# A three-block transformer kernel on one core: VectorE keeps the running sums of its depthwise convolution in PSUM

## The chip, the cores and the metric

The kernel runs on one core of a Trainium2 chip. The metric is the device time of one execution in microseconds (us), median of several runs. PE is the matrix engine (TensorE), DVE is VectorE, ACT is ScalarE, POOL is GpSimd, SP issues most DMAs. SBUF is the large on-chip memory, PSUM the eight banks of 128 partitions x 2 KB into which PE writes its sums.

## The reference

A sequence of 512 tokens of width 1024 goes through three layers, all in float32: one with a short convolution and latent attention, one with a conformer convolution (each of these two followed by a squared-ReLU MLP), and one with forgetting attention, pooling and a gated MLP. The change lies in the second:

```
def conformer_conv(h, w_pw1, b_pw1, w_dw, b_dw, ln_g, ln_b, w_pw2, b_pw2):
    u = h @ w_pw1 + b_pw1
    a, g = jnp.split(u, 2, axis=-1)
    u = a * jax.nn.sigmoid(g)
    u = depthwise_conv(u, w_dw) + b_dw      # 31 taps along the tokens, per channel
    u = jax.nn.silu(layer_norm(u, ln_g, ln_b))
    return u @ w_pw2 + b_pw2
```

## The kernel before, in words

Activations lie with 128 channels on the partitions and the 512 tokens along a partition, so the width of 1024 is eight channel tiles, c = 0 to 7. Every product is made of three fp32r matmuls of a head and a rest (`mm3`, L336 to L338). Weights are streamed: SP loads raw blocks, ACT makes the head (L264), DVE the rest (L265, which reads the raw block and the head, both in SBUF). Three raw buffers hold two blocks each; splitting is at most a few blocks ahead of PE.

In `conformer`, PE computes for each channel tile the two halves `za` and `zg` of `pw1` (two PSUM banks). `glu` then multiplies both by the norm's factor (DVE L1136, L1137: PSUM and SBUF in, SBUF out), ACT takes the sigmoid, and DVE L1139 makes the padded tile `up` of 542 tokens in SBUF from two SBUF tiles. The convolution of the tile is shared out by the string `CONV = "VPVVPMEE"`:

- V (c = 0, 2, 3): DVE does all 31 taps. The first is a multiplication (L1087), each later one `dst = u * w + dst` (L1091, called a tap below), where `u` is a shifted view of `up`, `w` one weight per partition, and `dst` the output tile `vv[c]` in SBUF.
- P (c = 1, 4): ACT multiplies (L1099 the first, L1102 the others, into a small buffer of a pool of nine), POOL adds the product to `vv[c]` (L1103).
- M (c = 5): ten taps as P, the other 21 on DVE into a tile `part` in SBUF (L1089, then L1091), and DVE adds the two (L1171, the merge).
- E (c = 6, 7): PE, as matmuls with diagonal matrices. `up` is split into head and rest (ACT L1109, DVE L1110). The diagonals of c = 6 are made earlier, those of c = 7 by ACT (L1060) during this stage. ACT L1129 takes the sum out of PSUM.

The taps are background work. DVE's are in the list `bg`, those of ACT and POOL in `bg2`; `tick(n, n2)` takes n and n2 operations, in turn from the first two tiles of a list, after each half of a `pw1` tile and each group of diagonals, and `drain` takes the rest. When all eight tiles `vv` are there, the layer norm begins: PE sums them over the channels (L1179, in the order 0, 2, 6, 1, 7, 4, 3, 5), DVE subtracts the mean, ACT squares (L1194), PE sums the squares (L1195), for the two halves of the tokens one after the other. The PSUM pool has eight banks.

The taps on DVE before:

```
else:
    V.scalar_tensor_tensor(out=dst, in0=u, scalar=w, in1=dst, op0=OP.mult, op1=OP.add)
```

Of the kernel before, what the change touches and what calls it, by code (L numbers as in the profile page):

```python
# [21 lines left out]
T = 512  # L22
# [41 lines left out]
# ---------------------------------------------------------------- host layout  # L64
# [12 lines left out]
def make_plan():  # L77
    """Weight pieces in the order in which they are used: (matrix, k, column tile, width)."""
# [64 lines left out]
def steps(order):  # L143
    """The steps of an order as it is written: name or name*times."""
    for s in order.split():
        name, _, n = s.partition("*")
        for _ in range(int(n or 1)):
            yield name


def pieces(order, use):
    """Weight pieces in the order of the steps that use them first."""
    use = {name: list(u) for name, u in use.items()}
    return sum([use[name].pop(0) for name in steps(order) if use.get(name)], [])


def pack(plan):
    """Cuts the plan into blocks of up to 512 columns, and those into loads of two blocks, but for the first two."""
    blocks, cols = [[]], 0
    for piece in plan:  # L160
        if cols + piece[3] > 512:
            blocks.append([])
            cols = 0
        blocks[-1].append(piece)
        cols += piece[3]
    return [blocks[:1], blocks[1:2]] + [blocks[i:i + 2] for i in range(2, len(blocks), 2)]
# [57 lines left out]
# ---------------------------------------------------------------- chip  # L224


class Weights:
    """Streams the weight blocks in and splits each into a 12 bit head and the exact rest."""
# [40 lines left out]
    def more(self, limit):  # L269
        """Splits one block beyond what is due, up to a number of blocks ahead."""  # L270
        if self.nsplit < min(self.cur + 1 + limit, len(self.blocks)):
            self.advance(self.nsplit - self.AHEAD)
# [10 lines left out]
class Program:  # L283
# [10 lines left out]
    # -- storage  # L294
# [23 lines left out]
    def tick(self, n, n2):  # L318
        """Background work: n and n2 operations of the two lists of queues, from a list's first two in turn."""
        for qs, num in ((self.bg, n), (self.bg2, n2)):  # L320
            for i in range(num):
                while qs and not qs[0]:
                    qs.pop(0)
                if not qs:
                    break
                q = qs[1] if i % 2 and len(qs) > 1 and qs[1] else qs[0]
                q.pop(0)()
# [5 lines left out]
    # -- arithmetic  # L333
# [6 lines left out]
    def units(self, name, t, xs, ks=None):  # L340
        """One closure (ps, columns) per product of a weight piece."""
# [13 lines left out]
    def kouter(self, names, h, ps=None, cols=slice(0, T), hooks=None, extra=None, ks=None):  # L355
        """Several output tiles at once, an input tile after the other."""
# [13 lines left out]
    def split(self, p, src, scale=None, cols=T, rows=slice(0, 128)):  # L370
        """p = (head, rest) of src [* scale per partition]."""
# [12 lines left out]
    def rsqrts(self, jobs):  # L384
        """out = (s / n + eps) ** -0.5, with one Newton step, for each (s, n, out)."""
# [23 lines left out]
    # -- tables of the scalar engine  # L409
# [4 lines left out]
    def tables(self, name):  # L414
        """Has the scalar engine load a set of tables, behind the functions that need the one before."""
# [10 lines left out]
    def fn(self, name, **args):  # L426
        """An activation whose function needs a set of tables."""
        self.tables(name)
        ins = self.nc.scalar.activation(**args).ins  # L429
        if self.table_load is not None:  # L430
            self.after(ins, self.table_load)
        self.table_fns.append(ins)

    def colsum(self, acc, cols=T):
        """Sums of acc over the partitions, on every partition."""
# [19 lines left out]
    # -- constants  # L455
# [13 lines left out]
    def late_consts(self):  # L469
# [14 lines left out]
        # a query on the partitions, a key on the columns: later keys are out  # L484
# [4 lines left out]
        # a key on the partitions, a query on the columns: 32 queries before the first 96 keys,  # L489
        # which stand above the 32 keys before them  # L490
# [6 lines left out]
        # a key of the last 32 on the first partitions, a query on the columns  # L497
# [4 lines left out]
        # adds the second 32 partitions to the first  # L502
# [11 lines left out]
    def angles(self):  # L514
        """cos and sin of the rope angles, row p for frequency p % 16."""
# [23 lines left out]
    # -- attention parts that both blocks use  # L539
# [7 lines left out]
    def v_tile(self, ps, rows, scales=None):  # L547
        """Values of four (block, head) groups as [v | ones | v | ones ...], head and rest."""
# [19 lines left out]
    def max_rows(self, mx, q, rows):  # L568
        """Puts the negative of the row maxima (mx[:, 4 * head + block]) into a row of each q."""
# [13 lines left out]
    def head_jobs(self, q, slots, scale, engines):  # L583
        """Closures of one head: scores and exponentials per slot of keys, then values.
        A slot is a list of (keys, first query, mask or None, values' function), where keys are the products
        (stationary, plane of q) that make the scores."""
# [5 lines left out]
        def score(j):  # L592
            ps = self.PS()
            off = 0
            for keys, c0, mask, _ in slots[j]:
                o = ps[:, off:off + T - c0]
                m = keys[0][0].shape[-1]
                # few keys: a first mask opens all the rows
# [32 lines left out]
    def normalise(self, e, o):  # L631
        """Values of a pair of heads over their sums: the even head is on top of its sums, the odd below."""
# [5 lines left out]
        # the negative of 1 / s, with one Newton step  # L638
# [8 lines left out]
    def head_ops(self, job, ys, nslots):  # L647
        """Closures for the scores and for the values of the slots of all heads; job(n) gives head n."""
# [20 lines left out]
    def parts(self, name, t, xs, done, ks=None, step=2):  # L669
        """A product in closures of a few input tiles each; done(sums) runs after the last."""  # L670
# [15 lines left out]
    # -- block 1, layer 0, mixer  # L686
    def mla(self, first):
# [10 lines left out]
        # products of constants until the first data is there: they raise the array's clock  # L698
# [68 lines left out]
        # shared key rope on partitions 64..95  # L767
# [6 lines left out]
        # query rope, (head, frequency) on the partitions  # L774
# [15 lines left out]
        # rows of a head: (64 | rope 32 | -max or 1 | zeros) or (-max or 1 | zeros | rope 32 | 64)  # L790
# [114 lines left out]
    # -- residual and norms between the parts  # L905
    def boundary(self, x, m, acc, last, gi, nxt, first, extra=None):
        """The last three tiles of m, x += rms_norm(m, g[gi]) and the first tiles of the next part, in halves
        of the tokens: the norms of one half run next to the products of the other.
        first: names of the next part's first tiles.  Returns x, h (without its rstd), the first tiles' sums
        and a function that gives the rstd."""  # L910
# [83 lines left out]
    # -- squared relu mlp  # L994
# [45 lines left out]
    # -- conformer convolution  # L1040
    def diagonals(self, c, early):
        """The taps of a channel tile as diagonal matrices, head and rest: at once, or eight as they are used."""
# [33 lines left out]
    def conformer(self, x, h, ps4, rs, first):  # L1076
# [5 lines left out]
        def conv_dve(c, up, dst, taps, bias):  # L1082
            def tap(t):
                w, u = self.v("dw", 31 * c + t), up[:, t:t + T]
                if t == taps[0]:
                    if bias:
                        V.tensor_scalar(out=dst, in0=u, scalar1=w, scalar2=self.v("bdw", c), op0=OP.mult, op1=OP.add)  # L1087
                    else:
                        V.tensor_scalar(out=dst, in0=u, scalar1=w, scalar2=None, op0=OP.mult)  # L1089
                else:  # L1090
                    V.scalar_tensor_tensor(out=dst, in0=u, scalar=w, in1=dst, op0=OP.mult, op1=OP.add)  # L1091

            return [lambda t=t: tap(t) for t in taps]
# [37 lines left out]
        def glu(c, za, zg):  # L1131
# [11 lines left out]
            elif CONV[c] == "V":  # L1143
                self.bg.append(conv_dve(c, up, vv[c], range(31), True))
            elif CONV[c] == "M":
                part = self.S()[:, :T]
                self.bg2.append(conv_pool(c, up, vv[c], range(MIX)))
                self.bg.append(conv_dve(c, up, part, range(MIX, 31), False))
# [21 lines left out]
        for c, part in mixed:  # L1170
            V.tensor_add(out=vv[c], in0=vv[c], in1=part)  # L1171
        self.tables(RSQRT)
        # layer norm in halves of the tokens; the tensor engine has little else to do and adds float32 as it is
# [60 lines left out]
    # -- block 2  # L1234
    def meta_norm(self):
        """The meta tokens' first norm, complete: head and rest, channels on the partitions."""
# [11 lines left out]
        # the heads and 16 columns of zeros, the rests and as many  # L1248
# [7 lines left out]
        # tokens on the partitions, the rest zero: keys of two pairs and one tile of the pooled part  # L1256
# [4 lines left out]
    def meta_unit(self, ps, w, k):  # L1261
        """Tokens on the partitions; the second 32 partitions take the tokens' rests."""
# [7 lines left out]
    def forget_first(self):  # L1270
        """The keys of the meta tokens next to the first tiles' second half."""
# [10 lines left out]
    def forget(self, x, h, ps4, rs, pm2):  # L1282
        """Keys stand in tiles of 128: 96 in their order and the 32 before them; the first tile has the meta
        tokens and 16 empty keys there, and the last 32 keys are in a tile of their own, below 96 empty ones."""
# [14 lines left out]
        # the first plane has the head of a head's 64 and rows (-max | 1), twice (-1 | 8 cum), twice (8 cum | 1),  # L1299
        # a head and a rest each; the second plane has (rest | head) and (head | rest)  # L1300
# [81 lines left out]
        # z * rstd and its squares, split  # L1382
# [13 lines left out]
        # the meta tokens' keys, tokens on the partitions  # L1396
# [91 lines left out]
        # values of four heads  # L1488
# [165 lines left out]
    # -- gated mlp of block 2  # L1654
# [88 lines left out]
```

## Time and profile before

| | before |
|---|---|
| median of 3 runs (lowest to highest) | 1869.91 us (1869.52 to 1872.47) |
| span of the profiled execution, first to last instruction | 1867.9 us |
| the profiled execution's own time | not recorded apart from its span |
| PE busy | 1773.1 us (95%) |
| DVE busy | 1176.0 us (63%) |
| ACT busy | 828.6 us (44%) |
| POOL busy | 330.1 us (18%) |
| mean granted clock of PE | 0.973 |

The profile is of one execution, taken by the hardware profiler. A busy share is an average over the whole span; the slices and windows tell where an engine is busy. Times of instructions are durations; since an instruction may start before the one ahead of it has ended, the distance between two starts can be shorter. [...]

### The profile page before, as it was taken

Reading aid. Unit: us, or ns where it says so; the run is one execution under the profiler, and the core shown is the slowest. Engines: PE = TensorE matmul, PEld = TensorE weight load, DVE = VectorE, ACT = ScalarE, POOL = GpSimd, SP = SyncE. Lnnn points to the kernel's source line nnn. Section 1 sums busy time; section 2 is a strip of 40 time slices with the busy share of each in tenths; the row PEclk is TensorE's granted clock in tenths of the full one; section 3 lists DMA queues with packets and bytes.
Section 4 is the critical chain, followed back from the end, with each engine's and each line's share of the span. In section 5 each row is a group of like instructions: output and inputs, shape, how many; then the busy total and the mean of one; then the engine's idle time right before and its main releaser. Section 6 shows DMA issues by size and latency. Waiting matters only on the chain.

```text
span 1867.9 us, 22812 instructions
## 1 busy us (share of the span) xinstructions
PE 1773.1 (95%) x8630; PEld 1459.5 (78%) x8630; DVE 1176.0 (63%) x1786; ACT 828.6 (44%) x1531; POOL 330.1 (18%) x353
## 2 busy tenths in 40 slices
PE   9999979999999986839999999999999999999999
PEld 7778877888888865729888888887777888888887
DVE  7978695344444899985934443458988654344442
ACT  6546645333333544817644242436666433232231
POOL 3413270000000357820300000015122200000000
PEclk9999999999999998969999999999999999999999
DMA  5231313322222211002232232223221332332231
GB/s 200 70 96 50 102 46 113 99 93 90 101 92 79 86 39 55 14 22 69 91 100 94 90 102 90 93 87 104 59 81 53 117 102 90 94 98 91 93 99 57
DMA packets 47581, 158.83 MB, mean 85 GB/s; under 512 B 6592, under 2 KB 7040, under 8 KB 47472
## 3 DMA queue, kind: packets, MB, share of 16 engines
q1 hardware_dynamic: 45472, 152.31, 24.9%
q0 software_dynamic: 1936, 5.07, 0.9%
q8 instruction: 67, 1.10, 0.2%
q14 instruction: 42, 0.34, 0.1%
q10 hardware_dynamic: 64, 0.02, 0.0%
HBM read 149.86 MB, written 4.19 MB: 82 GB/s over the span
## 4 chain that ended last, share of the span: by engine, by line
PE 72%; DVE 20%; issue 3%; ACT 2%; POOL 1%; DMA 1%; SPq 0%; POOLq 0%; DVEq 0%; ACTq 0%
PE ps L337 23%; PE ps L336 23%; PE ps L338 23%; DVE P L1091 5%; DVE W L265 2%; DVE P L947 1%; DVE P L380 1%; DVE S L1091 1%; PE ps L602 1%; POOL P L950 1%; DVE S L1479 1%; ACT S L429 1%; DVE P L377 1%; DVE S L403 1%; PE ps L1195 1%
## 5 line engine op out<-in xcount | busy, mean ns | idle before, releaser
L338 PE MATMUL ps<-P,W 128*128 128x512 f32 (+1 forms) x2413 | 900.0, 373 | 16.6 <-DVE W L265 16.6
L337 PE MATMUL ps<-P,W 128*128 128x512 f32 (+1 forms) x2413 | 900.6, 373 | 8.5 <-DVE P L380 8.5
L336 PE MATMUL ps<-P,W 128*128 128x512 f32 (+1 forms) x2413 | 904.7, 375 | 2.2 <-ACT P L379 1.0
L265 DVE TENSOR_TENSOR W<-raw,W 128x512 fp32r<-128x512 f32 x546 | 399.0, 739 | 396.1 <-ACT W L264 391.9
L264 ACT ACTIVATE W<-raw 128x512 fp32r<-128x512 f32 x546 | 338.6, 629 | 681.0 <-PE ps L338 583.8
L338 PEld LDWEIGHTS ps<-P,W 128*128 128x128 f32 x2413 | 458.2, 190 | 105.4 <-DVE W L265 19.4
L337 PEld LDWEIGHTS ps<-P,W 128*128 128x128 f32 x2413 | 458.7, 190 | 95.1 <-DVE P L380 10.0
L336 PEld LDWEIGHTS ps<-P,W 128*128 128x128 f32 x2413 | 458.6, 190 | 90.2 <-ACT P L379 1.6
L950 POOL TENSOR_TENSOR P<-P 128x256 f32<-128x256 f32 x48 | 46.6, 979 | 798.7 <-DVE P L947 797.6
L377 DVE TENSOR_TENSOR P<-S,P 128x512 fp32r<-128x512 f32 (+1 forms) x130 | 91.0, 706 | 50.1 <-ACT P L376 49.3
L1103 POOL TENSOR_TENSOR P<-P,S 128x512 f32<-128x512 f32 x69 | 113.8, 1670 | 49.0 <-ACT S L1102 47.6
L1091 DVE SCALAR_TENSOR_TENSOR P<-P,vec 128x512 f32<-128x512 f32 x90 | 112.3, 1288 | 0.0
L376 ACT ACTIVATE P<-S 128x512 fp32r<-128x512 f32 (+1 forms) x130 | 78.9, 613 | 70.2 <-DVE S L1666 25.8
L1008 DVE SCALAR_TENSOR_TENSOR S<-ps,S 128x512 f32<-128x512 f32 x64 | 43.7, 690 | 37.3 <-PE ps L338 37.1
L379 ACT ACTIVATE P<-P,vec 128x256 fp32r<-128x256 f32 (+1 forms) x80 | 43.7, 550 | 50.3 <-POOL P L950 30.4
L449 POOL TENSOR_TENSOR S<-S 128x256 f32<-128x256 f32 (+1 forms) x45 | 48.1, 1070 | 76.3 <-ACT S L448 73.9
L380 DVE SCALAR_TENSOR_TENSOR P<-P,vec 128x256 fp32r<-128x256 f32 (+1 forms) x80 | 55.9, 712 | 8.3 <-ACT P L379 8.2
L336 PE MATMUL ps<-P 128*128 128x512 f32 (+4 forms) x134 | 53.0, 395 | 7.3 <-ACT P L1060 3.3
L337 PE MATMUL ps<-P 128*128 128x512 f32 (+4 forms) x134 | 53.3, 398 | 4.2 <-DVE P L1110 3.8
L338 PE MATMUL ps<-P 128*128 128x512 f32 (+4 forms) x134 | 52.9, 395 | 1.6 <-ACT P L1060 1.6
L615 POOL TENSOR_TENSOR P<-S,P 128x512 fp32r<-128x512 f32 (+1 forms) x24 | 34.3, 1428 | 112.5 <-DVE P L614 95.6
L448 ACT ACTIVATE S<-P 128x256 f32<-128x256 f32 (+1 forms) x105 | 46.4, 472 | 17.4 <-DVE P L1035 11.4
(270 smaller groups left out, 1464.2 us busy)
## 6 DMA issues: line engine op xcount, KB each, us to landing
raw<-in_w SPq DMA_DIRECT2D x270, 512.0 KB
P<-in_xT SPq DMA_DIRECT2D x8, 256.0 KB
P<-in_xT POOLq DMA_DIRECT2D x8, 256.0 KB, 5.7
keep<-P SPq DMA_DIRECT2D x8, 256.0 KB
P<-P SPq DMA_DIRECT2D x16, 128.0 KB
P<-keep POOLq DMA_DIRECT2D x8, 256.0 KB, 4.9
out<-P SPq DMA_DIRECT2D x7, 256.0 KB
raw<-in_w SPq DMA_DIRECT2D x2, 256.0 KB
```

What stands on the lines that cost most here:

```text
L264: nc.scalar.activation(out=w[:, 0, :cols], in_=r, func=AF.Copy)
L265: nc.vector.tensor_sub(out=w[:, 1, :cols], in0=r, in1=w[:, 0, :cols].bitcast(F32))
L336: mm(ps, w[0], x[0], start=first, stop=False)
L337: mm(ps, w[0], x[1], start=False, stop=False)
L338: mm(ps, w[1], x[0], start=False, stop=last)
L376: nc.scalar.activation(out=hi, in_=src, func=AF.Copy)
L377: nc.vector.tensor_sub(out=lo, in0=src, in1=hi.bitcast(F32))
L380: nc.vector.scalar_tensor_tensor(out=lo, in0=src, scalar=scale, in1=hi.bitcast(F32), op0=OP.mult, op1=OP.subtract)
L449: (eng or nc.vector).tensor_add(out=acc, in0=acc, in1=t)
L950: ins = eng.tensor_add(out=x[k][:, cols], in0=x[k][:, cols], in1=m[k][:, cols]).ins
L1091: V.scalar_tensor_tensor(out=dst, in0=u, scalar=w, in1=dst, op0=OP.mult, op1=OP.add)
L1103: G.tensor_add(out=dst, in0=dst, in1=p)
```

## The change

`conv_dve` takes a bank of the PSUM pool when a tile's first tap is issued and keeps the running sum there. The first tap writes the bank, every further tap reads and writes it, and only the last tap of a V tile writes `vv[c]` in SBUF. The M tile has no buffer `part` any more: its sum stays in PSUM, and the merge reads it there. The rest of the diff strips comments, and every line behind `conv_dve` is numbered higher by 6 (L1091 becomes L1096, L1087 and L1089 become L1091 and L1093; L1102, L1103 become L1108, L1109; L1110 L1116; L1136 L1142; L1171 L1177; L1179 L1185).

```diff
         def conv_dve(c, up, dst, taps, bias):
+
+            box = {}
+
             def tap(t):
                 w, u = self.v("dw", 31 * c + t), up[:, t:t + T]
                 if t == taps[0]:
+                    acc = box["acc"] = self.PS()
                     if bias:
-                        V.tensor_scalar(out=dst, in0=u, scalar1=w, scalar2=self.v("bdw", c), op0=OP.mult, op1=OP.add)
+                        V.tensor_scalar(out=acc, in0=u, scalar1=w, scalar2=self.v("bdw", c), op0=OP.mult, op1=OP.add)
                     else:
-                        V.tensor_scalar(out=dst, in0=u, scalar1=w, scalar2=None, op0=OP.mult)
+                        V.tensor_scalar(out=acc, in0=u, scalar1=w, scalar2=None, op0=OP.mult)
                 else:
-                    V.scalar_tensor_tensor(out=dst, in0=u, scalar=w, in1=dst, op0=OP.mult, op1=OP.add)
-
-            return [lambda t=t: tap(t) for t in taps]
+                    acc = box["acc"]
+                    V.scalar_tensor_tensor(out=dst if dst is not None and t == taps[-1] else acc, in0=u, scalar=w,
+                                           in1=acc, op0=OP.mult, op1=OP.add)
+
+            return [lambda t=t: tap(t) for t in taps], box
...
             elif CONV[c] == "V":
-                self.bg.append(conv_dve(c, up, vv[c], range(31), True))
+                self.bg.append(conv_dve(c, up, vv[c], range(31), True)[0])
             elif CONV[c] == "M":
-                part = self.S()[:, :T]
                 self.bg2.append(conv_pool(c, up, vv[c], range(MIX)))
-                self.bg.append(conv_dve(c, up, part, range(MIX, 31), False))
+                taps, part = conv_dve(c, up, None, range(MIX, 31), False)
+                self.bg.append(taps)
                 mixed.append((c, part))
...
         for c, part in mixed:
-            V.tensor_add(out=vv[c], in0=vv[c], in1=part)
+            V.tensor_add(out=vv[c], in0=part["acc"], in1=vv[c])
```

The order on DVE at the end of the convolution, from the second L1110 (after: L1116) on, before the change (P and S are tiles in SBUF, ps is a PSUM bank, vec the weights per partition; the last two rows shown then go on in turn up to the merge):

```order
L1110 TENSOR_TENSOR P<-P 128x542
L1091 SCALAR_TENSOR_TENSOR P<-P,vec 128x512 x15
L1089 TENSOR_SCALAR S<-P,vec 128x512
L1091 SCALAR_TENSOR_TENSOR P<-P,vec 128x512 x4
L1091 SCALAR_TENSOR_TENSOR S<-P,vec,S 128x512
L1091 SCALAR_TENSOR_TENSOR P<-P,vec 128x512
```

and of the change:

```order
L1116 TENSOR_TENSOR P<-P 128x542
L1096 SCALAR_TENSOR_TENSOR ps<-P,vec,ps 128x512 x13
L1093 TENSOR_SCALAR ps<-P,vec 128x512
L1096 SCALAR_TENSOR_TENSOR P<-P,vec,ps 128x512
L1096 SCALAR_TENSOR_TENSOR ps<-P,vec,ps 128x512 x41
L1177 TENSOR_TENSOR P<-ps,P 128x512
L1096 SCALAR_TENSOR_TENSOR P<-P,vec,ps 128x512
L265 TENSOR_TENSOR W<-raw,W 128x512 x3
```

The number of taps is the same; three more of them stand ahead of the second L1116, and the merge now stands one tap before the last.

The order on ACT from the last tile's sigmoid (L429) to the diagonals of c = 7 (`wh` and `wl` are the weights' heads and rests), before the change:

```order
L429 ACTIVATE S<-S,vec 128x512
L1102 ACTIVATE S<-P,vec 128x512 x3
L1109 ACTIVATE P<-P 128x542
L1102 ACTIVATE S<-P,vec 128x512 x4
L1060 ACTIVATE P<-ident,wh_2642 128x128 x8
L1060 ACTIVATE P<-ident,wl_2643 128x128 x8
```

and of the change:

```order
L429 ACTIVATE S<-S,vec 128x512
L1108 ACTIVATE S<-P,vec 128x512 x2
L1115 ACTIVATE P<-P 128x542
L1108 ACTIVATE S<-P,vec 128x512 x19
L1060 ACTIVATE P<-ident,wh_2642 128x128 x8
L1060 ACTIVATE P<-ident,wl_2643 128x128 x8
```

Nineteen products for POOL stand between the last tile's head and the first diagonals, where four stood.

## Rows read from the trace of the kernel before

**Rows 1.** Page, part 2: PE's busy tenths in 40 slices of 46.7 us.
```profile
PE   9999979999999986839999999999999999999999
```

**Rows 2.** Windows: us, each engine's busy time (instructions), PEclk, DMA share, GB/s.
```profile
655.46:760.94 105.48, 84.16 (x320) 65.43 (x319) 105.48 (x98) 50.95 (x86) 71.88 (x54) 0.89 0.14 45
760.94:796.40 35.46, 30.51 (x120) 23.90 (x119) 35.46 (x24) 33.13 (x83) 32.81 (x21) 0.90 0.00 0
```

**Rows 3.** PE's waits from 640 to 870: total us, times, longest.
```profile
PE ps L1179 <- DVE P L1091: 19.9, 1, 19.9
...
PE ps L1179 <- POOL P L1103: 7.7, 1, 7.7
```

**Rows 4.** Groups by shape on DVE, 655.46 to 827.83: busy us, mean ns, idle before.
```profile
L1091 DVE SCALAR_TENSOR_TENSOR P<-P,vec 128x512 f32<-128x512 f32 x90 | 112.3, 1288 | 0.0
L1091 DVE SCALAR_TENSOR_TENSOR S<-P,vec,S 128x512 f32<-128x512 f32 x20 | 19.9, 993 | 0.0
L265 DVE TENSOR_TENSOR W<-raw,W 128x512 fp32r<-128x512 f32 x19 | 19.8, 1076 | 0.0
L1139 DVE SCALAR_TENSOR_TENSOR P<-S,vec 128x512 f32<-128x512 f32 x8 | 10.1, 1261 | 0.0
L1136 DVE TENSOR_TENSOR S<-ps,S 128x512 f32<-128x512 f32 x8 | 5.4, 678 | 0.0
...
L1110 DVE TENSOR_TENSOR P<-P 128x542 fp32r<-128x542 f32 x2 | 3.6, 1798 | 0.0
```

**Rows 5.** Timelines of POOL and DVE where POOL's adds end: start us, duration us.
```profile
784.59 21.56 POOL L1103 TENSOR_TENSOR P<-P,S 128x512 f32<-128x512 f32 x13
...
804.95 1.75 DVE L1091 SCALAR_TENSOR_TENSOR S<-P,vec,S 128x512 f32<-128x512 f32 x1
806.62 0.74 DVE L1091 SCALAR_TENSOR_TENSOR P<-P,vec 128x512 f32<-128x512 f32 x1
807.28 0.74 DVE L1091 SCALAR_TENSOR_TENSOR S<-P,vec,S 128x512 f32<-128x512 f32 x1
```

**Rows 6.** Timelines of POOL and DVE about 750.
```profile
749.95 3.05 POOL L1103 TENSOR_TENSOR P<-P,S 128x512 f32<-128x512 f32 x1 [2.51 <-ACT S L1102]
...
750.57 1.28 DVE L265 TENSOR_TENSOR W<-raw,W 128x512 fp32r<-128x512 f32 x2
751.77 0.67 DVE L1136 TENSOR_TENSOR S<-ps,S 128x512 f32<-128x512 f32 x1
752.38 0.67 DVE L1137 TENSOR_TENSOR S<-ps,S 128x512 f32<-128x512 f32 x1
```

**Rows 7.** Timeline of PE in c = 7's convolution, at low and at full clock.
```profile
786.21 0.63 PE L338 MATMUL ps<-P 128*128 128x512 f32 x1
...
787.91 0.63 PE L336 MATMUL ps<-P 128*128 128x512 f32 x1
...
790.07 0.40 PE L337 MATMUL ps<-P 128*128 128x512 f32 x1
...
792.40 0.40 PE L338 MATMUL ps<-P 128*128 128x512 f32 x1
```

**Rows 8.** Timeline of ACT: eight diagonals, and ten products for POOL.
```profile
758.93 2.44 ACT L1060 ACTIVATE P<-ident,wh 128x128 fp32r<-128x128 f32 x8
...
767.14 6.23 ACT L1102 ACTIVATE S<-P,vec 128x512 f32<-128x512 f32 x10
```

**Rows 9.** All of one line: duration ns min/median/max, first and last start.
```profile
L1103 POOL TENSOR_TENSOR P<-P,S x69: 1287/1708/3048, 661.5 to 804.6; 128x512 f32<-128x512 f32 x69
...
L1087 DVE TENSOR_SCALAR P<-P,vec x3: 532/535/1701, 660.4 to 753.6; 128x512 f32<-128x512 f32 x3
```

**Rows 10.** Window before the layer norm (as rows 2), and the chain from there.
```profile
820.00:830.00 10.00, 2.07 (x4) 1.16 (x4) 9.17 (x15) 0.38 (x1) 0.00 (x0) 0.50 0.05 12
...
830.86 6.66 PE ps L1195 x16
...
848.65 3.50 PE ps L1195 x16
```

## The prediction

> **What bounds the kernel now.** Over the whole span it is PE; only in one place do the slices show it idle [rows 1]: PE's digits fall to 8, 6, 8, 3 in the four slices of 46.7 us from 654 us on. That is the conformer's convolution. By windows DVE is busy for all of 105.48 and 35.46 us, and no group of its instructions up to 827.8 has idle time before it [rows 2, 4]: it never waits. PE's 440 matmuls in these two windows would take 440 x 0.233 us = 103 us at the full clock (ten of them go by in 2.33 us [rows 7]), and they take 141, because they wait for DVE; behind them PE waits 19.9 us for DVE's last tap and 7.7 us for POOL's last add, which ends with DVE's turns, below [rows 3]. So the stretch is worth what DVE is worth.
>
> What fills DVE is the 110 taps, 112.3 + 19.9 us [rows 4], and they have two speeds. As long as POOL's adds run, one tap starts 1.67 us after the other; from the moment they stop, at 806.15, a tap of the same shape starts every 0.66 us [rows 5]. POOL's 13 adds take 21.56 us there, 1.66 each: the two engines go in turn, each standing still while the other works, 0.66 for the tap and 1.0 for the add. Not every DVE instruction does that. At 749.95 an add of POOL is stretched to 3.05 us: it stood still through two L265, then ran beside L1136 and L1137, which took 0.67 us each, no more than without POOL [rows 6]. L265, L1110 and L1139 read two tiles of SBUF, as a tap does, and are the ones with means of 1.08, 1.80 and 1.26; L1136, which reads one tile from PSUM and one from SBUF, keeps to 0.678 over all eight [rows 4]. So **a tap loses its 1.0 us because both its tiles are in SBUF.** The change puts one of them into PSUM.
>
> **The change part by part.** *The taps.* Pitch is the time from one start to the next, on DVE 0.08 less than a duration (0.66 against 0.74 [rows 5]). The 110 taps take 123 us now: 132.2 less 110 x 0.08 [rows 4]. Each will read `u` from SBUF and the sum from PSUM. No DVE instruction of the kernel before writes PSUM, so that has no row. Below, the nearest is the pitch of L1136, 0.60 [rows 6]. Above, I take the tap's whole duration with nothing overlapped, 0.74, and add once more the 0.06 by which a tap's pitch exceeds L1136's: 0.80. I take 0.70, the middle, since the tap alone has 0.66 and reading PSUM costs L1136 nothing against L265 (both 0.60 apart when undisturbed [rows 6]). 110 x 0.70 = 77 us.
>
> [...]
>
> *The rest of DVE's list in the stretch*, by pitch: 16 multiplications of the gate x 0.60 = 9.6; 8 L1139, which still read two SBUF tiles, x (1.26 - 0.08) = 9.4; 4 first taps x 0.60 = 2.4; 17 L265 x (1.08 - 0.08) = 17; 2 L1110 x 1.7 = 3.4; the merge 0.6. With the taps 119 us, and DVE is done at 655.5 + 119 = **775** in place of 827.8: 53 us less. At 0.60 it would be 764, at 0.80 786. (The same list with 123 for the taps and 4 for the first taps gives 167 of the 172.3 us that it took; the 5 left I take to belong to the turns.)
>
> *PSUM.* At most two sums are open at once, with the four banks of `za` and `zg` six of eight. The only new wait of PE is that of the third pair's bank on the first gate multiplication, at 656, before PE needs it. I cost it at nothing.
>
> *PE.* When DVE is done with the gates, c=6 and c=7 remain. By the same pitches DVE has 79 us up to its second L1110 (54 taps, 3 first taps, 17 L265, the gates), so that lies at 734, and the first, 14 us or so earlier, at 720. From there 93 matmuls of c=6 last 22 us at full clock, those of c=7 as long, or 48 together at the 0.90 that PE was granted from 760.94 to 796.40 [rows 2]: 768, plus some 4 us wait for c=7's diagonals, 772. PE is three us under DVE: they are nearly even, and a further gain on DVE would find PE next.
>
> *ACT and POOL.* The ACT order puts 19 products (L1102, L1108 after the change) before c=7's first diagonals where 4 stood. A product takes some 0.62 us [rows 8], but needs a buffer that POOL's add gives back; with eight free at 733, the 19th waits for POOL's 11th add of that row, at 1.0 to 1.29 us each (1.0 from the turns above, 1.29 the shortest duration of any add [rows 9]) 744 to 747, and eight diagonals more, 2.4 us [rows 8], bring the first product of c=7 to 747 to 750. That is the 4 us wait or a little over it. POOL's 69 adds took 114 us in turns; without the taps it is 69 to 89 us of work, spread by its waits for ACT's products, done about 770: no longer last.
>
> *Layer norm.* [...] The 16 matmuls of the first half's squares took 6.66 us, those of the second half 3.50 [rows 10]. With a wait of some 3 us in the place of 20 the first half comes nearer to the second: I take 3 us of 4 (the means' four matmuls among it).
>
> *Sum*: 53 + 3 = 56 us of the span of 1867.9, 1811.9. The median of the runs, 1869.91, stands 2.0 above the span of the profiled execution, so **1814 us**.
>
> **Rivals.**
> 1. *The diagonals of c=7 set the end.* If PE's clock falls to the lower level in its waits for c=6 and c=7, as it did at 786 to 788 (four matmuls in 1.70 us, 0.43 each [rows 7]), the 93 matmuls of c=7 from 750 last 40 us, and the layer norm starts at 790: 38 us less than now, 1832. For it: three waits of PE on ACT's or DVE's late work lie here, and 15 more products stand before the diagonals. Against it: PE recovered within the same convolution before.
> 2. *A tap in PSUM takes 1.0 us.* Then 110 + 42 = 152 us, DVE done at 808, 20 us gained: 1850. For it: writing PSUM from DVE has no row, and each tap reads what the one before it, or the one before that, wrote. Against it: dependent taps two apart ran at 0.66 [rows 5].
> 3. *The lock stays.* The per-partition weight is read from SBUF too; if this counts as a second read, taps keep 1.67 beside POOL: 1870, no change. For it: L1087, with one tile and two such columns, once took 1.70 [rows 9]. Against it: its other two took 0.53, faster than any pitch of a two-tile instruction, so it reads its tile in a way of its own, which the same instruction into PSUM may lose.
> 4. *Slower.* A tap pays for PSUM twice in a row, one whole pitch to read and one to write, 2 x 0.66 = 1.32 us. Against the mean pitch now (123 / 110 = 1.12), that is 110 x 0.20 = 22 us more: 1892. It decides from 1.12 us a tap on. For it there is no row; against it the reading costs nothing [rows 6].
>
> **How the numbers follow.** My forecast has 0.74, rival 1 0.12, rival 2 0.05, rival 3 0.06, rival 4 0.03. In the forecast DVE's ends give 764 to 786, where PE holds the lower one at 768: 60 + 4 to 42 + 2 us less, 1806 to 1826. The range takes this and rival 1, and a few us below for products that come sooner: 1803 to 1834. A measurement of this kernel tells about 0.2%, 3.7 us, from no change. Faster by more than that: 0.74 + 0.12 + 0.05 = 0.91; within: 0.06; slower: 0.03.
>
> **What would show it.** In the profile after, taps with PSUM in and out of one duration near 0.75 to 0.80, whether POOL's adds run or not, and no second group at 1.75; adds of POOL at 1.0 to 1.3 except beside L265, L1110 and L1139; the last tap and the merge at 764 to 786; PE's 19.9 us wait for the last tap down to a few us; a wait of PE for a diagonal of ACT of about 4 us; the squares' first half nearer 4 us than 6.66. It is wrong if taps still have two speeds, if they are over 0.9 us, or if PE's last wait before the layer norm is on ACT or on its own clock.

## The result, and the profile after

The changed kernel takes 1813.49 us (median of 4 runs, 1813.39 to 1813.95), the kernel before 1870.91 us beside it: a ratio of 0.9693, 95% interval 0.9679 to 0.9706, 57 us less. In four later runs its median was 1812.97 us, a ratio of 0.9698 (0.9684 to 0.9712) to the kernel before beside it. The span of its profiled execution is 1810.8 us, against 1867.9. The forecast was 1814, with a range from 1803 to 1834.

The slices of PE and DVE and PE's granted clock (a share of its full speed, in tenths) on the page of the changed kernel, where [rows 1] stood:

```profile
PE   9999989999999998999999999999999999999999
...
DVE  7988687243444699967634444478997554344442
...
PEclk9999998999999999999999999999999999999999
```

The digits 8, 6, 8, 3 of [rows 1] are gone; in that place PE has one 8 and is at 9 otherwise. DVE is still close to full there, but for less long.

All taps (L1096) and all of POOL's adds (L1109) of the changed kernel, by line: duration in ns as least, median and longest, first and last start in us. They answer to [rows 4] and [rows 9].

```profile
L1096 DVE SCALAR_TENSOR_TENSOR ps<-P,vec,ps x107: 737/742/758, 662.7 to 769.6; 128x512 f32<-128x512 f32 x107
L1096 DVE SCALAR_TENSOR_TENSOR P<-P,vec,ps x3: 727/731/735, 725.2 to 770.9; 128x512 f32<-128x512 f32 x3
...
L1109 POOL TENSOR_TENSOR P<-P,S x69: 1264/1297/2142, 662.5 to 772.7; 128x512 f32<-128x512 f32 x69
```

The two speeds are gone: the slowest of 110 taps has 0.758 us, where about half of them had some 1.75 before. POOL's adds went from a median of 1.71 to 1.30 us. The two now run beside one another. DVE's timeline of the changed kernel (start, duration, with the count at the end of a line):

```profile
730.41 1.40 DVE L1096 SCALAR_TENSOR_TENSOR ps<-P,vec,ps 128x512 f32<-128x512 f32 x2
731.72 1.75 DVE L1116 TENSOR_TENSOR P<-P 128x542 fp32r<-128x542 f32 x1
733.40 8.64 DVE L1096 SCALAR_TENSOR_TENSOR ps<-P,vec,ps 128x512 f32<-128x512 f32 x13
741.96 0.74 DVE L1093 TENSOR_SCALAR ps<-P,vec 128x512 f32<-128x512 f32 x1
742.61 0.73 DVE L1096 SCALAR_TENSOR_TENSOR P<-P,vec,ps 128x512 f32<-128x512 f32 x1
743.27 27.08 DVE L1096 SCALAR_TENSOR_TENSOR ps<-P,vec,ps 128x512 f32<-128x512 f32 x41
770.26 0.67 DVE L1177 TENSOR_TENSOR P<-ps,P 128x512 f32<-128x512 f32 x1
770.86 0.73 DVE L1096 SCALAR_TENSOR_TENSOR P<-P,vec,ps 128x512 f32<-128x512 f32 x1
771.52 3.90 DVE L265 TENSOR_TENSOR W<-raw,W 128x512 fp32r<-128x512 f32 x3
```

and POOL's, of the same stretch:

```profile
730.09 28.59 POOL L1109 TENSOR_TENSOR P<-P,S 128x512 f32<-128x512 f32 x22 [0.33 <-ACT S L1108]
762.75 6.30 POOL L1109 TENSOR_TENSOR P<-P,S 128x512 f32<-128x512 f32 x5 [4.07 <-ACT S L1108]
769.93 4.34 POOL L1109 TENSOR_TENSOR P<-P,S 128x512 f32<-128x512 f32 x3 [0.88 <-ACT S L1108]
```

From 743.27 to 770.26 there are 41 taps, 0.658 us apart, with POOL's adds going on beside them: exactly the distance that a tap in SBUF had once POOL was still [rows 5]. L1116, which still reads two SBUF tiles, still takes 1.75. DVE is done with the last tap at 771.5, PE with its last convolution matmul at about 772.7, and POOL with its last add at 774.3: three engines end within three microseconds.

PE's waits between 640 and 870 us (total, times, longest), where [rows 3] stood:

```profile
PE ps L336 <- ACT P L1115: 4.2, 1, 4.2
PE ps L336 <- ACT P L1060: 2.1, 1, 2.1
PE ps L337 <- DVE P L1116: 1.7, 1, 1.7
...
PE ps L338 <- ACT P L1060: 1.1, 1, 1.1
```

and PE's timeline, its first matmuls of the layer norm, which answer to [rows 10]:

```profile
772.70 3.62 PE L1185 MATMUL ps<-P,onesf 128*128 128x256 f32 x16
777.82 3.72 PE L1201 MATMUL ps<-S,onesf 128*128 128x256 f32 x16 [1.50 <-ACT S L1200]
```

The waits of 19.9 and 7.7 us before the layer norm are gone. What is left are the waits for the head and the rest of c = 6 (4.2 and 1.7) and for the diagonals of c = 7 (2.1 and 1.1). After the last of these PE goes from the convolution straight into the layer norm, without a wait for DVE or POOL. So it is PE that sets the layer norm's start, 1.2 us after DVE's last tap. The chain of work that ended last (start, duration) shows what set PE's end: behind POOL's products on ACT the diagonals of c = 7, then PE's matmuls.

```profile
746.76 2.64 ACT P L1060 x9
749.45 0.79 PE ps L338
```

### The profile page after: what moved, and what is told of

Its sections match the earlier page's. It is cut to its first block, busy times and chain, and to the rows that moved or that the text cites. A ratio compares the mean times of both kernels' runs of the same rounds, so it can differ in the third digit from the quotient of the medians.

```text
span 1810.8 us, 22812 instructions
## 1 busy us (share of the span) xinstructions
PE 1760.7 (97%) x8630; PEld 1457.2 (80%) x8630; DVE 1122.1 (62%) x1786; ACT 828.6 (46%) x1531; POOL 312.0 (17%) x353
## 4 chain that ended last, share of the span: by engine, by line
PE 75%; DVE 16%; issue 4%; ACT 3%; POOL 1%; DMA 0%; SPq 0%; ACTq 0%; POOLq 0%; DVEq 0%
PE ps L337 24%; PE ps L336 24%; PE ps L338 24%; DVE W L265 3%; DVE ps L1096 2%; DVE P L947 1%; DVE P L380 1%; PE ps L602 1%; DVE P L377 1%; ACT S L429 1%; DVE S L1485 1%; POOL P L950 1%; DVE S L449 1%; DVE S L403 1%; DVE S L401 0%
## 5 line engine op out<-in xcount | busy, mean ns | idle before, releaser
L265 DVE TENSOR_TENSOR W<-raw,W 128x512 fp32r<-128x512 f32 x546 | 403.8, 748 | 395.1 <-ACT W L264 391.2
L264 ACT ACTIVATE W<-raw 128x512 fp32r<-128x512 f32 x546 | 338.3, 629 | 662.2 <-PE ps L338 582.7
L1109 POOL TENSOR_TENSOR P<-P,S 128x512 f32<-128x512 f32 x69 | 96.3, 1419 | 34.4 <-ACT S L1108 33.0
L1096 DVE SCALAR_TENSOR_TENSOR ps<-P,vec,ps 128x512 f32<-128x512 f32 x107 | 72.4, 743 | 0.0
```

Of the source, the lines that this page charges most:

```text
L264: nc.scalar.activation(out=w[:, 0, :cols], in_=r, func=AF.Copy)
L265: nc.vector.tensor_sub(out=w[:, 1, :cols], in0=r, in1=w[:, 0, :cols].bitcast(F32))
L1096: V.scalar_tensor_tensor(out=dst if dst is not None and t == taps[-1] else acc, in0=u, scalar=w, in1=acc, op0=OP.mult, op1=OP.add)
L1109: G.tensor_add(out=dst, in0=dst, in1=p)
```

## The experiments

Theory: DVE and POOL go in turn when a DVE instruction reads two SBUF tiles beside an add of POOL; a tap with its sum in PSUM reads one, and no longer does. First rival: it is where the sum is written that matters. Second rival: taps in SBUF are slow by themselves, or the order of the work made the gain.

**The sum only written to PSUM, both inputs in SBUF** (the sums are not carried from tap to tap):

```diff
...
-                    V.scalar_tensor_tensor(out=dst if dst is not None and t == taps[-1] else acc, in0=u, scalar=w,
-                                           in1=acc, op0=OP.mult, op1=OP.add)
+                    last = bias and t == taps[-1]
+                    V.scalar_tensor_tensor(out=dst if last else acc, in0=u, scalar=w,
+                                           in1=dst, op0=OP.mult, op1=OP.add)
...
```

The parts left out let the first taps write SBUF and give the M tile a buffer there.

> Every tap reads two SBUF tiles, as before, and writes a PSUM bank (the sums are not carried from tap to tap, so the convolution of the DVE tiles is not complete). Theory, two SBUF inputs make DVE and POOL go in turn: taps keep two speeds, about 1.67 us apart beside POOL's adds and 0.66 without, and the time stays near the kernel before, 1865 to 1875 us. Rival, it is the write into SBUF that collides: all taps 0.66 apart, some 1813 us.

It took 1873.45 us, the kernel before 1869.29 beside it (one run each, as in the next three experiments). DVE's timeline where POOL's adds end; the last 30 of them run from 763.42 to 813.80 us:

```profile
810.93 1.75 DVE L1097 SCALAR_TENSOR_TENSOR ps<-P,vec,S 128x512 f32<-128x512 f32 x1
812.60 1.75 DVE L1097 SCALAR_TENSOR_TENSOR ps<-P,vec 128x512 f32<-128x512 f32 x1
814.27 0.75 DVE L1097 SCALAR_TENSOR_TENSOR ps<-P,vec,S 128x512 f32<-128x512 f32 x1
814.93 0.75 DVE L1097 SCALAR_TENSOR_TENSOR ps<-P,vec 128x512 f32<-128x512 f32 x1
```

The taps write PSUM, and are 1.67 us apart beside POOL and 0.66 without, as in the kernel before. Where the sum is written is not what collides.

**The sum only read from PSUM, written to SBUF** (not carried either):

```diff
-                    V.scalar_tensor_tensor(out=dst if dst is not None and t == taps[-1] else acc, in0=u, scalar=w,
+                    V.scalar_tensor_tensor(out=dst, in0=u, scalar=w,
                                            in1=acc, op0=OP.mult, op1=OP.add)
...
```

The parts left out give the M tile a buffer in SBUF, which the merge reads.

> Every tap reads one SBUF tile and one PSUM bank and writes SBUF (again the sums are not carried from tap to tap). Theory, two SBUF inputs: all taps 0.66 apart, adds of POOL 1.25 to 1.3, 1810 to 1818 us. Rival, the write into SBUF: taps 1.67 apart beside POOL's adds, some 1870 us.

1810.67 us. The taps by form, from 655 to 830 us (busy us, mean ns, idle before):

```profile
L1096 DVE SCALAR_TENSOR_TENSOR P<-P,vec,ps 128x512 f32<-128x512 f32 x90 | 62.9, 739 | 0.0
...
L1096 DVE SCALAR_TENSOR_TENSOR S<-P,vec,ps 128x512 f32<-128x512 f32 x20 | 14.9, 743 | 0.0
```

One operand moved out of SBUF on the reading side is the whole effect. That settles the first rival, and it also rules out that the weight's column counts as a second read: here it is read from SBUF as before, and the taps keep one speed. Which part of the way into SBUF the two engines take turns at, no run shows.

**Without POOL's adds**, from the kernel before (POOL's share of the convolution is left out):

```diff
                 A.activation(out=p, in_=u, func=AF.Copy, scale=w)
-                G.tensor_add(out=dst, in0=dst, in1=p)
```

> The kernel before without POOL's 69 adds (the POOL share of the convolution is left out; ACT still makes the products). Theory: with nobody to take turns with, the 110 taps in SBUF are 0.66 apart, L265 0.60, L1110 0.62; DVE's list is 102 us, done about 757, and PE holds the layer norm to about 765: 1800 to 1810 us. Rival, taps in SBUF are slow for a reason of their own and PSUM mends that: two speeds stay, some 1870 us.

1796.48 us, with the taps in SBUF; groups on DVE from 655 to 790 us:

```profile
L1091 DVE SCALAR_TENSOR_TENSOR P<-P,vec 128x512 f32<-128x512 f32 x90 | 63.9, 760 | 0.0
L265 DVE TENSOR_TENSOR W<-raw,W 128x512 fp32r<-128x512 f32 x24 | 15.6, 691 | 0.1
...
L1109 DVE TENSOR_TENSOR P<-P 128x542 fp32r<-128x542 f32 x2 | 1.5, 727 | 0.0
```

Taps in SBUF are not slow by themselves. L265 and L1109 (the split of c = 6 and 7), which read two SBUF tiles, also fall to 0.69 and 0.73 us. PE now waits for nobody from 655 us up to the layer norm, which starts at 756.3. The expectation, 1800 to 1810, was 3.5 us too high at its lower end, as PE had been put at 765; so this run, 17 us below the changed kernel, is about the floor that PE alone sets here.

**Without DVE's taps**, from the changed kernel (the trace has 3 taps left of 110, so 107 are left out, and not the 104 of the expectation):

```diff
-                    V.scalar_tensor_tensor(out=dst if dst is not None and t == taps[-1] else acc, in0=u, scalar=w,
-                                           in1=acc, op0=OP.mult, op1=OP.add)
+                    if bias and t == taps[-1]:
+                        V.scalar_tensor_tensor(out=dst, in0=u, scalar=w, in1=acc, op0=OP.mult, op1=OP.add)
```

> The changed kernel with only the first and the last tap of the three V tiles and the first of M (104 taps left out). Theory, a tap on PSUM does not touch POOL: POOL's adds keep the 1.25 us distance that they have in the changed kernel, and the layer norm starts where PE and POOL let it, 760 to 768: 1797 to 1808 us. Rival, taps on PSUM still slow POOL: adds about 1.0 us apart and POOL done 15 us earlier.

1802.99 us. POOL's timeline in the longest run of adds:

```profile
723.96 28.31 POOL L1109 TENSOR_TENSOR P<-P,S 128x512 f32<-128x512 f32 x22 [1.61 <-ACT S L1108]
```

22 adds take 28.31 us with two taps beside them, and 28.59 in the changed kernel with some 40 (one L1116 lies beside either row). POOL does not feel taps on PSUM. An add by itself thus takes 1.29 us of POOL, where 1.0 was read from the turns before.

**M's sum back in SBUF**, the V tiles as changed:

```diff
...
-                taps, part = conv_dve(c, up, None, range(MIX, 31), False)
+                part = self.S()[:, :T]
...
+                        V.scalar_tensor_tensor(out=part, in0=u, scalar=w, in1=part, op0=OP.mult, op1=OP.add)
...
```

> The changed kernel with the sum of c=5 (M) back in SBUF; the V tiles stay in PSUM. Theory: M's 20 taps read two SBUF tiles again and lie in the last 30 us, beside POOL's adds; each costs 1.0 us more while adds run, DVE is done up to 20 us later and the time is 1825 to 1834 us. Rival, the gain comes from the order of the work and not from single taps: near 1813 us.

1819.45 us (one run), 6 us above the changed kernel: the direction of the theory, but half its size or less (1825 to 1834 were expected). DVE's timeline, in which M's taps (L1160) and those of c = 3 (L1096) alternate:

```profile
757.64 1.13 DVE L1160 SCALAR_TENSOR_TENSOR S<-P,vec,S 128x512 f32<-128x512 f32 x1
758.70 0.74 DVE L1096 SCALAR_TENSOR_TENSOR ps<-P,vec,ps 128x512 f32<-128x512 f32 x1
759.36 1.13 DVE L1160 SCALAR_TENSOR_TENSOR S<-P,vec,S 128x512 f32<-128x512 f32 x1
```

and POOL's:

```profile
728.00 47.10 POOL L1109 TENSOR_TENSOR P<-P,S 128x512 f32<-128x512 f32 x30 [0.62 <-ACT S L1108]
```

and PE's, where it waits for both:

```profile
775.15 1.22 PE L1194 MATMUL ps<-P,onesf 128*128 128x256 f32 x2 [6.11 <-POOL P L1109]
777.62 2.08 PE L1194 MATMUL ps<-P,onesf 128*128 128x256 f32 x4 [1.25 <-DVE P L1096]
```

An SBUF tap costs 1.06 us here and not 1.67. The numbers fit this reading: POOL's add uses the 0.66 us of the PSUM tap ahead of it, and the SBUF tap waits only for the rest of the add, 0.4 us. 20 x 0.4 is 8 us more for DVE. POOL's adds go at the pace of the pair while the two kinds of taps alternate, 1.7 us, and PE waits first for POOL and then for DVE. So the price of a tap in SBUF depended on what stood before it on DVE: 1.06 us behind a tap on PSUM, 1.67 behind another tap in SBUF [rows 5].

**Shifting the shares.** Since three engines end together in the changed kernel and PE's floor is 17 us lower, four variants change the constants of the shares alone; the first of them:

```diff
-MIX = 10
+MIX = 14
...
-TICK = (5, 4)
+TICK = (4, 5)
```

> The changed kernel with TICK = (4, 5) in place of (5, 4) and MIX = 14 in place of 10: fewer taps stand ahead of the gates of c=6 and c=7, POOL gets its products earlier, and four taps go from DVE to POOL. Theory, after the change PE, DVE and POOL end within 3 us of each other, and PE alone could be done 14 us earlier: some of PE's 9 us of waits go, 1806 to 1811 us. Rival, one of the three is the bound and the others follow: 1813 us or more.

> As v1_tick45_mix14, with TICK = (4, 6): POOL's products come earlier still and fewer are left behind the diagonals of c=7. Theory: 1804 to 1810 us, if POOL's idle time (33 us in the changed kernel) is what holds its end. Rival, more of POOL's adds in the loop meet L265, which still reads two SBUF tiles, and DVE is later by as much: 1811 to 1815 us.

They took 1816.82 us (ratio to the kernel before 0.9706, 0.969 to 0.9722) and 1823.16 us (0.9755, 0.9732 to 0.9778): the first is no gain (its interval overlaps the changed kernel's 0.9679 to 0.9706), the second a loss. The rivals' side was right, but the second lies 8 us above even its rival's range, and mostly by another wait than named. PE's waits with TICK = (4, 6), 650 to 800 us:

```profile
PE ps L336 <- ACT P L1115: 15.6, 1, 15.6
PE ps L336 <- ACT P L1060: 2.2, 1, 2.2
```

L1115 makes c = 6's head on ACT. From 699 us on POOL adds without a pause, 25 times and then 24, so POOL is never short. The products for it stand in ACT's queue and wait for POOL's buffers; DVE waits 6.7 us for heads of weights (L264) that stand behind them. Late by this, and by more turns with POOL (L1145 takes 1.16 us in the mean, where it takes 0.74 in the changed kernel), DVE has the tile of c = 6 (L1145) ready only at 726.9 us, and PE, which had been done with `pw1` since 712, waits 15.6 us for its head.

> The changed kernel once more, beside the two that follow: 1813 to 1815 us.

> The changed kernel with TICK = (4, 4): one tap fewer per half of a pw1 tile, POOL's share as it was. In the changed kernel a pw1 tile has some 12.4 us of DVE work and 11.2 us of PE work; with eight taps in place of ten it is 11.1 against 11.2. Theory: PE's waits for the gates of c=6 (4.2 and 1.7 us) go, DVE's list is as long as before and still ends about 771: 1809 to 1813 us. Rival, PE's wait for c=6 was the bound itself: 1806 to 1808 us.

> As v7_tick44, with MIX = 14: four taps of 0.66 us leave DVE, and POOL gets four adds of 1.25 us. Theory, DVE is the last by a little: 1806 to 1811 us. Rival, POOL's end moves back by as much: 1811 to 1815 us.

The three ran side by side: the changed kernel 1812.97 us (0.9698, 0.9684 to 0.9712), TICK = (4, 4) 1816.5 (0.9718, 0.97 to 0.9736), and with MIX = 14 as well 1819.97 (0.9738, 0.9719 to 0.9756). Both variants lie above the theory's and the rival's range; the first is no gain, the second a loss. PE's matmuls of the layer norm with TICK = (4, 4):

```profile
764.45 2.32 PE L1185 MATMUL ps<-P,onesf 128*128 128x256 f32 x10
768.09 0.70 PE L1185 MATMUL ps<-P,onesf 128*128 128x256 f32 x2 [1.31 <-POOL P L1109]
772.47 2.07 PE L1185 MATMUL ps<-P,onesf 128*128 128x256 f32 x4 [3.68 <-DVE P L1096]
776.04 6.69 PE L1201 MATMUL ps<-S,onesf 128*128 128x256 f32 x16 [1.50 <-ACT S L1200]
```

PE is done with the convolution 8 us sooner and POOL 6 us (2 of these from an earlier start of the stretch), and it brings nothing, because now PE waits for DVE, whose last tap lands at 772.4. DVE's list was expected to be as long as in the changed kernel. It is 118.0 us and not 115.1, because four L265 (the split of weights), which stand behind the last tap in the changed kernel, stand among the last taps here and cost 3.7 us; two rows of DVE's timeline:

```profile
764.11 1.12 DVE L265 TENSOR_TENSOR W<-raw,W 128x512 fp32r<-128x512 f32 x1
768.51 3.12 DVE L1096 SCALAR_TENSOR_TENSOR ps<-P,vec,ps 128x512 f32<-128x512 f32 x4
```

PE, which waited, ran the squares of the first half in 6.69 us where it took 3.72 in the changed kernel. What this share would be worth with the four L265 behind the taps, no run shows. The four taps that MIX = 14 takes from DVE did not help either: DVE's merge stands in front of the other taps and waits 6.6 us for POOL's longer share, as this row of DVE's timeline shows.

```profile
774.42 0.69 DVE L1177 TENSOR_TENSOR P<-ps,P 128x512 f32<-128x512 f32 x1 [6.61 <-POOL P L1109]
```

None of the four variants beats the changed kernel.

## Why the prediction was right

The time (1814 against 1813.5) came out, and the mechanism of the gain, that a tap takes turns with POOL because both its tiles are in SBUF, is shown from both sides by the runs with the sum only written to PSUM (taps 1.67 us apart beside POOL) and only read from it (taps of 0.739 and 0.743 us in the mean). That the number is so close is partly luck, as two errors cancel, and one sign that the prediction had named as speaking against it did appear: PE's last wait before the layer norm is on ACT, for a diagonal of c = 7, and not on DVE. (The same list had also foreseen a wait of about 4 us there; 2.1 + 1.1 came.) The prediction had DVE's end at 775 and PE's at 772, "nearly even". They came at 771.5 and 772.7, in the other order, since DVE's list was 4 us shorter than summed. So the last microsecond belongs to the path of the first rival, at nothing like its price. The terms, one by one:

- *Taps.* 0.70 was forecast, 0.66 measured, at 110 taps 72.4 us and not 77. Reading and writing PSUM cost a tap nothing beyond SBUF: 742 ns is the median duration with PSUM in and out, 0.74 us the duration with all in SBUF [rows 5]. The taps are 0.66 apart from start to start, and one that reads PSUM and writes SBUF takes 739 ns on average in the run with the sum only read from PSUM, no more than with all in SBUF.
- *The rest of DVE's list.* 42 us were forecast and 43 measured, but two terms missed in opposite ways. L1145 (L1139 before) was taken with its old mean of 1.26 us; all eight began in pauses of POOL and took at most 0.746, 5.3 us together from start to start and not 9.4. The 17 L265 were taken at 1.0 apart and came to 21 us, not 17: POOL is in an add more often when one of them starts (it is busy for 79% of the time from 656 to 733 us, and was for 68% up to 761 [rows 2]). (The group below has four more, which stand outside the list.) The sum of these, 115 us for the list, against 119.

```profile
L1145 DVE SCALAR_TENSOR_TENSOR P<-S,vec x8: 736/742/746, 658.2 to 729.7; 128x512 f32<-128x512 f32 x8
...
L265 DVE TENSOR_TENSOR W<-raw,W 128x512 fp32r<-128x512 f32 x21 | 26.4, 1292 | 0.0
```

- *DVE's end.* 771.5 from a start at 656.45, one us later than in the kernel before; 775 was forecast. By the list that is 57 us less, not 53.
- *PE and the diagonals.* Of the 38 us that PE's matmuls took beyond full clock in the kernel before, 20 were waits for DVE; 6 were waits for ACT, and 12 went at the lower clock (0.89 and 0.90 granted [rows 2]). The prediction put all of them down to DVE. In the changed kernel c = 6 was forecast to start at 720, and its first two matmuls stand at 718.6 and 720.7; c = 7's first product at 747 to 750, and it stands at 747.1. PE's end, 772, came out. PE's clock did fall to the lower level behind the waits for both tiles, as the first rival had it: matmuls are 0.43 us apart from 721.3 to 726.0 and again from 750.0 to 753.0, and the granted clock is 0.62 from 718 to 727 us and from 745 to 754 (0.50 from 721.3 to 725.5 and from 750 to 753), 1.00 in between and afterwards. But it came back after a dozen of them. In all this cost some 5 us, about the 4 that the prediction had charged (48 us for 44), where the rival would have had 18 for c = 7 alone.
- *POOL.* Its end was put at 770, "no longer last", and is 774.3, the last of the three; but PE did not wait for it. The 1.0 us for an add came from the turns; by itself an add takes 1.29.
- *Layer norm.* This term failed: 3 us were counted for the squares of the first half, an estimate of the author's from the 6.66 and 3.50 us of the two halves [rows 10]. They did get shorter by 2.9 us (3.72 against 6.66): over them PE's granted clock was 0.54 in the kernel before (0.50 from 820 to 830 us, while PE waited [rows 10]) and 1.00 in the changed kernel. But from DVE's end to the first of them 6.3 us pass (771.52 to 777.82) where 3.1 did (827.76 to 830.86). Before, PE had done 12 of the 16 matmuls of the sums while it waited, as the two rows show; now it is in the convolution until 772.7, and all 16 (3.62 us) come after DVE's end. Gain and loss cancel. It had been forecast that "a further gain on DVE would find PE next"; the term should have been charged with that.

```profile
796.15 2.32 PE L1179 MATMUL ps<-P,onesf 128*128 128x256 f32 x10
806.20 1.22 PE L1179 MATMUL ps<-P,onesf 128*128 128x256 f32 x2 [7.73 <-POOL P L1103]
```

So 53 + 3 stood where 57 + 0 came out; the sum was nearer than its parts. (The stretch began 1 us later than in the kernel before, and 1 us more was gained behind the layer norm.)

The rivals: that a tap in PSUM takes 1.0 us or is paid for twice fell to the 0.742 us; that the lock stays because of the weight's column fell to the run with PSUM only read.

## What to carry to other kernels

When an instruction of DVE shows two clearly parted durations in one shape, the longer while POOL is busy, ask whether it takes turns with POOL, as the taps did here (1.67 against 0.66 us); both engines lost by it here, 1.0 us a tap and 0.38 us an add. Look at how many of its inputs are in SBUF, and compare with a neighbour that reads one from PSUM. A running sum can stand in a PSUM bank if banks are free, here at no cost to a tap; what counted here was where it was read from (1.67 us from tap to tap beside POOL with the sum only written to PSUM, a mean duration of 0.74 us with it only read there). And once a bound goes, ask how far behind the next engines are: here PE and POOL ended 1 to 3 us after DVE, and the four ways of shifting shares between them that were run brought nothing.

## What had not been expected of the hardware

In turns, a tap and an add take 1.67 us together, while alone they take 0.66 and 1.29, 1.95 in sum: some 0.28 us of each pair do overlap. The turns cost DVE 1.0 us a tap, but POOL only 0.38 us an add. A first tap, the multiplication into PSUM, is 0.81 us (741.96 in the list above has 0.74 for the one without a bias), where it took 0.53 into SBUF beside no add [rows 9]; with four of them this is about 1 us.

```profile
L1091 DVE TENSOR_SCALAR ps<-P,vec 128x512 f32<-128x512 f32 x3 | 2.4, 809 | 0.0
```

With TICK = (4, 4) the last taps are all of one tile, and each reads the sum that the tap just before it wrote. Four such taps in a row are 0.79 us apart (768.51 above, the next at 771.66), where taps of two tiles in turn are 0.66 apart. No run changes this alone.
